# Probabilities times values in pairs of float16, in a two-layer attention and recurrence trunk on one Trainium2 core

## The chip, the cores and the metric

The kernel runs on one core of a Trainium2 chip. The metric is the device time of one execution in microseconds (us). Five engines work side by side, each with its own queue of instructions: TensorE (PE in the profile; its weight loads are PEld), VectorE (DVE), ScalarE (ACT), GpSimd (POOL) and SyncE (SP), which here only issues transfers.

## The reference

A sequence of 512 tokens with 16 meta tokens ahead of it (528 in all, width 2048) goes through an even layer (a convolution module and sparse attention side by side, then one output projection) and an odd layer (a gated linear recurrence). The change lies in the attention. For each of 8 heads, and for blocks of 128 queries:

```python
score = einsum('bqh,bqhs->bqs', wi_b, relu(dots))            # the indexer
_, idx = top_k(where(admissible, score, NEG_INF), topk)      # 128 keys for each query
logits = einsum('bqhc,bqkc->bhqk', q_b, c_sel) + bias
p = softmax(where(valid, logits, NEG_INF), axis=-1)
o = einsum('bhqk,bqkc->bhqc', p, c_sel)                      # probabilities times values
...
b_out = einsum('bthc,hcd->bthd', o_lat, w_uv) * silu(gate_b)
y = concatenate([a_out, b_out]) @ w_out
```

The kernel multiplies the latent keys by the up-projections first, so that each head has keys and values of width 128, and keeps the selection as a mask over all keys up to the block's chunk.

## The kernel before

A float32 operand is split into two float16 tiles, a high half (scaled, by ScalarE) and a low half (the rest, by VectorE, which therefore waits for the high half), and a main product is three float16 matmuls into the same PSUM tile: high by high, high by low, low by high. `products` (lines 214 to 216) does this for the projections; I call its three matmuls a main triple. Weights come in tiles of 2048 columns (`load_two`): SyncE loads `w`, ScalarE makes `wh` (L174), VectorE makes `wl` (L175), with three buffers each. Some weights are sums formed in DRAM by GpSimd's transfers (`ws`, L287 and L289), which are issued a few at a time behind steps of the attention.

The even layer runs through the table `EVEN`: `g` is a stripe of the convolution module, `s` a pair of indexer heads, `k` the selection of 128 keys for one block, `h` an attention head, `n` the layer norm. For head `h`, `head` computes gate and query, and every second head `keys_values` makes keys and values for two heads: five blocks of keys (the 16 meta keys, and four of 128), six float16 matmuls each, into one PSUM tile of 256 columns, 128 for each head, from which ScalarE evicts one head at a time (L555) into `Vt`.

`attend` then takes four blocks of queries, t = 0 to 3. For each, `softmax` makes the scores (L717), adds the bias and takes the extreme (L720, VectorE), takes the exponential (L724) and divides by the sum (L727, both ScalarE). The probabilities are transposed by TensorE in blocks of 128 keys into one PSUM tile for the t + 1 blocks (L736) and another for the meta keys (L740), evicted by ScalarE (L737, L741) into `pt` in float32, and multiplied by the values in float32 (L743), t + 2 products into `o`. After four blocks VectorE multiplies `o` by the gate (L754), and SyncE stores the result to `mbd` in DRAM (L755). `attend_meta` does the same for the meta queries of all heads at once (L679, L681).

Behind the eighth head come eight more gates (`GA`), and then the output projection, whose operands B21 and B22 are the heads' results read back from `mbd` (L852) and split (L234, L235; `fh`, `fl`).

Work is recorded in the order of the code, with priorities: `WGT` (weights) above `EVAC` (evictions of main products) above `SIDE` (attention) above `CONV` (the convolution's 31 steps on `z`, L632). A scheduler then sets each engine's order from its own estimates of times, so that a change in one part moves others. Each engine works strictly in its order.

Of the kernel before, what the change touches and what calls it, by code (L numbers as in the profile page):

```python
# [19 lines left out]
NM = 16  # L20
# [15 lines left out]
LEVELS = (1, 2, 4, 8, 16, 32, 64)  # L36

KS, QS = 2.0 ** 14, 1.0
WS = 2.0 ** 10
IW = 1.0 / WS  # L40

EROLE = {"gt": "em", "gb": "em", "qh": "em", "rstd": "em", "u": "em",
         "z": "ec", "acc": "ec", "sq": "ec",
         "Kh": "ek", "Vt": "ek",
         "wiT": "ei", "ki": "ei", "rt": "ei", "m8": "ei",
         "mask0": "ei", "mask1": "ei", "mask2": "ei", "mask3": "ei"}

# [27 lines left out]
def trunk_kernel(ctx: ExitStack, tc: tile.TileContext, x: bass.AP, w: bass.AP, wukv: bass.AP,  # L75
# [308 lines left out]
    def split_weights(s, half, part=None):  # L384

        m = KWM if s == S_KW else 128
        if s not in raw:
            raw[s] = raw_tile()
            if s == S_KW:
                first[s] = [[et([128, 5, 128], F32, *at).rearrange("p a b -> p (a b)").bitcast(F16)[:, :640]  # L390
                             for _ in range(2)] for at in (("Vt", 3), ("pt", 2))]
            else:
                first[s] = both_halves(*weight_tiles())
        hi, lo = first[s][half]
        w32 = raw[s][:, half * 1024:(half + 1) * 1024]
        cs = slice(0, 8 * m) if part is None else slice(4 * m * part, 4 * m * (part + 1))
        Q.dma_start(w32[:, cs], w[s, half, :, cs])
        in_turn("a", lambda: S.activation(hi[:, cs], w32[:, cs], AF.Copy, scale=WS))
        in_turn("v", lambda: V.scalar_tensor_tensor(lo[:, cs], w32[:, cs], WS, hi[:, cs],
                                                    op0=OP.mult, op1=OP.subtract))  # L400
# [124 lines left out]
    def keys_values(pr):  # L525
        with band(WGT):
            hi, lo = [E.tile([128, 2 * T], F16, name=n, bufs=1)[:, :1024] for n in ("uh", "ul")]
            split2(hi, lo, kvw.pop(), WS)
        Ks = []
        for hh in range(2):  # L530
            Kh = et([128, T], F32, "Kh", 3)
            for half in range(2):
                sl = slice(half * HT, half * HT + HT)
                p = ps1()
                n = 0
                for k in range(2):
                    ws = slice((2 * hh + k) * 128, (2 * hh + k + 1) * 128)
                    for a, b in ((hi, 0), (hi, 1), (lo, 0)):
                        P.matmul(p[:, :HT], a[:, ws], CX[k][b][:, sl], start=n == 0, stop=n == 5)
                        n += 1  # L540
                S.activation(Kh[:, sl], p[:, :HT], AF.Copy, scale=128.0 ** -0.5 * IW)
            Ks.append(Kh)
        Vs = [et([128, 5, 128], F32, "Vt", 3) for _ in range(2)]
        for Vh in Vs:
            G.memset(Vh[:, 0, :], 0.0)
        for i, (s0, ns) in enumerate(blocks):
            p = ps1()
            n = 0
            for k in range(2):
                ws = slice(512 + k * 256, 512 + (k + 1) * 256)  # L550
                for a, b in ((hi, 0), (hi, 1), (lo, 0)):
                    P.matmul(p[:ns, :256], CX[k][b][:, s0:s0 + ns], a[:, ws], start=n == 0, stop=n == 5)
                    n += 1
            for hh in range(2):
                S.activation(Vs[hh][:ns, i, :], p[:ns, hh * 128:(hh + 1) * 128], AF.Copy, scale=IW)  # L555
        if pr < HB // 2 - 1:
            load_keys_values(pr + 1)
        return Ks, Vs


    M = []
# [90 lines left out]
    def meta_tiles():  # L652

        t = epools["ei"].tile([128, 4, 128], F32, name="ql", bufs=1)
        for i, name in enumerate("qkvg"):
            meta[name] = t[:, i, :]
        meta["b"] = epools["ei"].tile([128, 128], F32, name="wiT", bufs=1)
        with band(SIDE):
            G.memset(meta["b"], NEG)
            for h in range(HB):  # L660
                G.dma_start(meta["b"][h * NM:(h + 1) * NM, h * NM:(h + 1) * NM], bias_rows(h, 0, NM, 0, NM))

    def attend_meta():

        e = et([128, T], F32, "sq", 3)
        L = e[:, :128]
        st = et([128, 4], F32, "st", 3)
        p = ps1()
        P.matmul(p[:, :128], meta["q"], meta["k"], start=True, stop=True)
        V.tensor_tensor_reduce(L, p[:, :128], meta["b"], -1.0, BIG, OP.add, OP.min, st[:, 0:1])  # L670
        S.activation(L, L, AF.Exp, bias=st[:, 0:1], scale=-1.0, accum_out=st[:, 2:3])
        V.reciprocal(st[:, 3:4], st[:, 2:3])
        S.activation(L, L, AF.Identity, scale=st[:, 3:4])
        p = ps1()
        P.transpose(p[:, :128], L, ident)
        pt = et([128, 5, 128], F32, "pt", 2)
        S.activation(pt[:, 0, :], p[:, :128], AF.Copy)
        p = ps1()
        P.matmul(p[:, :128], meta["v"], pt[:, 0, :], start=True, stop=True)  # L679
        mb = spare()  # L680
        V.tensor_tensor(mb[:, :128], p[:, :128], meta["g"], op=OP.mult)  # L681
        Q.dma_start(mbd[:, :, :NM].rearrange("h p t -> p h t"), mb[:, :128].rearrange("p (h t) -> p h t", h=HB))

    biased = {}
# [12 lines left out]
    def attend(h, qh, gb, Kh, Vt):  # L697
        o = pso()
        both = E.tile([128, 2 * T], F16, name=("uh", "ul")[h % 2], bufs=1)
        kr = both[:, :T], both[:, T:]  # L700
        both = (et([128, CW - 1 + T], F32, "u", 2) if h >= HB - 2 else et([128, T], F32, "acc", 2)).bitcast(F16)
        qr = both[:, :SEQ], both[:, SEQ:2 * SEQ]
        split2(*kr, Kh)
        split2(*qr, qh[:, NM:])

        def softmax(t, nq, q0, W):
            if h == 0:
                bias_ahead(h, t)
                some_steps(gsteps, 6, mask_ahead(h, t))
            e = biased.pop((h, t))  # L710
            L = e
            st = et([128, 4], F32, "st", 3)
            parts = ((0, W),) if W <= 512 else ((0, HT), (HT, W))
            for i, (s0, s1) in enumerate(parts):
                p = ps1()
                for a, b in ((0, 0), (0, 1), (1, 0)):
                    P.matmul(p[:nq, :s1 - s0], qr[a][:, q0 - NM:q0 - NM + nq], kr[b][:, s0:s1],  # L717
                             start=a + b == 0, stop=a == 1)

                V.tensor_tensor_reduce(L[:nq, s0:s1], p[:nq, :s1 - s0], e[:nq, s0:s1], -1.0,  # L720
                                       st[:nq, i - 1:i] if i else BIG, OP.add, OP.min,
                                       st[:nq, i:i + 1])
            i = len(parts) - 1
            S.activation(L[:nq, :W], L[:nq, :W], AF.Exp, bias=st[:nq, i:i + 1], scale=-1.0,  # L724
                         accum_out=st[:nq, 2:3])
            V.reciprocal(st[:nq, 3:4], st[:nq, 2:3])
            S.activation(L[:nq, :W], L[:nq, :W], AF.Identity, scale=st[:nq, 3:4])  # L727
            return L

        for t in range(NB):  # L730
            q0, W = NM + 128 * t, wk(t)
            L = softmax(t, 128, q0, W)
            pt = et([128, 5, 128], F32, "pt", 2)
            p = ps1()
            for j in range(t + 1):
                P.transpose(p[:, j * 128:(j + 1) * 128], L[:, NM + 128 * j:NM + 128 * (j + 1)], ident)  # L736
            S.activation(pt[:, 1:t + 2, :], p[:, :128 * (t + 1)], AF.Copy)  # L737

            p = ps1()
            P.transpose(p[:, :128], L[:, :128], ident)  # L740
            S.activation(pt[:, 0, :], p[:, :128], AF.Copy)  # L741
            for j in range(t + 2):
                P.matmul(o[:, 128 * t:128 * (t + 1)], Vt[:, j, :], pt[:, j, :],  # L743
                         start=j == 0, stop=j == t + 1)
            if h < HB - 1:
                behind = bias_ahead(h + 1, t)
                if t:
                    mask = mask_ahead(h + 1, t - 1)
                    behind = behind if h else mask
                some_steps(steps, (2, 2, 2, 3)[t] if h == 0 else (2, 2, 1, 2)[t] if h < 6 else 1, behind)  # L750
                if t == NB - 1:
                    mask_ahead(h + 1, t)
        mb = spare()
        V.tensor_tensor(mb[:, NM:], o, gb[:, NM:], op=OP.mult)  # L754
        Q.dma_start(mbd[h, :, NM:], mb[:, NM:])  # L755

    def head(h):
# [14 lines left out]
        with band(SIDE):  # L772
            for name, src in (("q", qh), ("k", Kh), ("g", gb)):
                S.activation(meta_of(name, h), src[:, :NM], AF.Copy)
            moved = G.dma_start(meta["v"][h * NM:(h + 1) * NM, :], Vt[:NM, 0, :])
            if h == HB - 1:
                some_steps(gsteps, 7, moved)
            if h == HB - 1:
# [896 lines left out]
```

## Time and profile before

| | us |
|---|---|
| median of 3 runs | 1742.28 |
| lowest, highest | 1742.22, 1743.06 |
| the profiled execution | 1739.7 |
| its span in the trace | 1737.9 |
| busy in the span: PE, PEld, DVE, ACT, POOL | 1720.5, 1457.2, 1401.3, 949.5, 271.3 |

The granted TensorE clock is 0.998 over the span. Lines of the page and of the trace name an instruction by its source line, its engine and its tiles, written as out<-in; buffer numbers are left out. Idle time of an engine that nobody waits for costs nothing.

### The profile page before, as it was taken

What the parts mean: (1) busy time and instruction counts of PE and PEld (TensorE: products, weight loads), DVE (VectorE), ACT (ScalarE), POOL (GpSimd) and SP (SyncE); (2) the same over time, 40 slices, a digit from 0 to 9 for tenths busy, and PEclk for the clock granted to TensorE, in tenths of its full rate; (3) what the DMA queues carried; (4) which work ended last, traced back from release to release, by engine and by line L of the source; (5) the groups of instructions that cost most, each with busy time, mean ns of one, the idle gap of its engine ahead of it and who ended that gap; (6) DMA issues with size and microseconds to landing.
All of it is one profiled execution on the core that took longest, in us unless ns stands there. A gap on an engine that the chain in (4) does not pass through costs nothing.

```text
span 1737.9 us, 38189 instructions
## 1 busy us (share of the span) xinstructions
PE 1720.5 (99%) x15784; PEld 1457.2 (84%) x15784; DVE 1401.3 (81%) x2362; ACT 949.5 (55%) x1745; POOL 271.3 (16%) x485
## 2 busy tenths in 40 slices
PE   9999999999999999999999999999999999999997
PEld 8775588888888888888888888899989989857886
DVE  7699899999569569689876667888878787759876
ACT  7333542224544555466644355778767777646553
POOL 1021233113343212010200111111111010000000
PEclk9999999999999999999999999999999999999999
DMA  9579677979999957887789987665555554424764
GB/s 368 150 253 262 193 236 186 263 206 243 246 245 303 219 192 251 252 285 260 228 287 309 297 269 242 190 181 172 141 176 157 153 165 134 123 85 170 255 223 141
DMA packets 103870, 378.53 MB, mean 218 GB/s; under 512 B 14096, under 2 KB 21944, under 8 KB 101840
## 3 DMA queue, kind: packets, MB, share of 16 engines
q1 hardware_dynamic: 70496, 232.68, 38.0%
q0 software_dynamic: 32912, 143.23, 33.9%
q8 instruction: 123, 2.02, 0.5%
q14 instruction: 51, 0.42, 0.1%
q10 hardware_dynamic: 288, 0.19, 0.0%
HBM read 354.26 MB, written 136.53 MB: 282 GB/s over the span
## 4 chain that ended last, share of the span: by engine, by line
PE 83%; DVE 10%; issue 3%; DMA 3%; ACT 1%; POOL 0%; SPq 0%; DVEq 0%; POOLq 0%; ACTq 0%
PE mps L216 18%; PE mps L214 18%; PE mps L215 18%; PE s L216 2%; PE s L215 2%; PE s L214 2%; DVE wl L175 2%; DVE z L632 2%; DVE mask L606 1%; PE sv L216 1%; PE sv L215 1%; PE sv L214 1%; PE po L743 1%; DVE m L605 1%; PE st L216 1%
## 5 line engine op out<-in xcount | busy, mean ns | idle before, releaser
L215 PE MATMUL mps<-xl,wh 128*128 128x264 f16 (+2 forms) x2840 | 806.0, 284 | 0.1
L216 PE MATMUL mps<-xh,wl 128*128 128x264 f16 (+2 forms) x2840 | 805.9, 284 | 0.1
L214 PE MATMUL mps<-xh,wh 128*128 128x264 f16 (+2 forms) x2840 | 805.8, 284 | 0.0
L175 DVE SCALAR_TENSOR_TENSOR wl<-w,wh 128x2048 f16<-128x2048 f32 (+1 forms) x188 | 429.1, 2282 | 136.6 <-ACT wh L174 136.1
L174 ACT ACTIVATE wh<-w 128x2048 f16<-128x2048 f32 (+1 forms) x188 | 357.6, 1902 | 304.1 <-PE mps L215 197.7
L216 PEld LDWEIGHTS <-wl 128*128 128x128 f16 x4184 | 409.4, 98 | 81.0 <-DVE wl L175 2.3
L215 PEld LDWEIGHTS <-wh 128*128 128x128 f16 x4184 | 409.4, 98 | 77.8 <-issue 0.6
L214 PEld LDWEIGHTS <-wh 128*128 128x128 f16 x4184 | 409.3, 98 | 77.6 <-issue 0.4
L632 DVE SCALAR_TENSOR_TENSOR z<-u,vec,z 128x528 f32<-128x528 f32 x240 | 179.5, 760 | 2.1
L289 POOL DMA_DIRECT2D ws<-in_w_dram x116 | 105.1, 1110 | 113.8 <-DMA ws<-ws 64.7
L216 PE MATMUL s<-xh,wl 128*128 128x256 f16 (+1 forms) x288 | 78.8, 274 | 0.0
L214 PE MATMUL s<-xh,wh 128*128 128x256 f16 (+1 forms) x288 | 78.8, 274 | 0.0
L215 PE MATMUL s<-xl,wh 128*128 128x256 f16 (+1 forms) x288 | 78.8, 274 | 0.0
L1242 ACT ACTIVATE kt1h<-k 128x512 f16<-128x512 f32 x64 | 41.2, 644 | 31.3 <-DVE k L1309 22.8
L1309 DVE TENSOR_TENSOR k<-k,e 128x512 f32<-128x512 f32 (+1 forms) x80 | 55.7, 696 | 1.4
L695 POOL DMA_DIRECT2D L<-mask x32 | 30.0, 939 | 160.0 <-DMA L<-bdram 89.5
L1243 DVE TENSOR_TENSOR kt1l<-k,kt1h 128x512 f16<-128x512 f32 x64 | 44.0, 687 | 12.1 <-ACT kt1h L1242 11.9
L222 DVE SCALAR_TENSOR_TENSOR gt<-mps,rstd 128x264 f32<-128x264 f32 (+1 forms) x70 | 31.3, 447 | 25.5 <-PE mps L216 24.5
L1243 DVE TENSOR_TENSOR kt0l<-k,kt0h 128x512 f16<-128x512 f32 x48 | 33.9, 707 | 17.7 <-ACT kt0h L1242 17.6
L724 ACT ACTIVATE L<-L,st 128x144 f32<-128x144 f32 (+3 forms) x32 | 18.4, 574 | 50.5 <-DVE st L720 50.2
L287 POOL DMA_DIRECT2D ws<-ws x58 | 36.5, 649 | 60.6 <-DMA ws<-in_w_dram 55.1
L1242 ACT ACTIVATE kt0h<-k 128x512 f16<-128x512 f32 x48 | 32.8, 683 | 17.7 <-DVE k L1309 17.2
(637 smaller groups left out, 3208.3 us busy)
## 6 DMA issues: line engine op xcount, KB each, us to landing
w<-in_w_dram SPq DMA_DIRECT2D x86, 1024.0 KB, 7.3
ws<-in_w_dram POOLq DMA_DIRECT2D x158, 512.0 KB, 7.9
w<-ws SPq DMA_DIRECT2D x116, 512.0 KB, 4.9
w<-in_w_dram SPq DMA_DIRECT2D x90, 512.0 KB, 4.8
ws<-ws POOLq DMA_DIRECT2D x58, 512.0 KB, 5.2
ws<-in_w_dram SPq DMA_DIRECT2D x16, 512.0 KB, 7.9
on<-h1d SPq DMA_DIRECT2D x30, 256.0 KB, 5.3
sq<-mbd POOLq DMA_DIRECT2D x16, 264.0 KB, 4.3
```

Of the source, the lines that this page charges most:

```text
L174: halved[:] = [S.activation(hi[:, :n], w32[:, :n], AF.Copy, scale=WS), V.scalar_tensor_tensor(lo[:, :n], w32[:, :n], WS, hi[:, :n], op0=OP ...
L175: V.scalar_tensor_tensor(lo[:, :n], w32[:, :n], WS, hi[:, :n], op0=OP.mult, op1=OP.subtract)]
L214: P.matmul(o, hi[:, ws], xh, start=start and k == 0, stop=False)
L215: P.matmul(o, hi[:, ws], xl, start=False, stop=False)
L216: issued.append(P.matmul(o, lo[:, ws], xh, start=False, stop=stop and k == len(X) - 1))
L222: V.scalar_tensor_tensor(dst[:, sl.start - o:sl.stop - o], p[:dst.shape[0]], IW, rstd[:dst.shape[0], sl], op0=OP.mult, op1=OP.mult)
L287: return (Q if m in (5, 7) and pair in EPAIRS else G).dma_start(dst, src)
L289: return G.dma_start(wsum[pair, m], src, accum_op=OP.add, max_dma_last_dim=4096)
L632: V.scalar_tensor_tensor(z, u[:, j:j + T], col(V_CW + i * CW + j), z, op0=OP.mult, op1=OP.add)
L1242: S.activation(hi, src, AF.Copy)
L1243: V.tensor_tensor(lo, src, hi, op=OP.subtract)
L1309: V.tensor_tensor(both, both, by, op=OP.mult)
```

## The change

Values are kept as two float16 tiles `Vh` and `Vl`, each of 256 columns for two heads, so one split evicts both heads at once. Probabilities are split at their eviction into `ph` and `pl`, scaled by 1024, which the outputs' eviction takes out again. Each float32 product becomes three float16 ones. For t = 0 to 2 the meta keys are transposed into the same PSUM tile as the others and share their eviction; for t = 3, which has 512 other columns, they keep their own. The meta queries' values are copied in two transfers for each head instead of one.

```diff
+PS = 2.0 ** 10
...
-        Vs = [et([128, 5, 128], F32, "Vt", 3) for _ in range(2)]
+        Vs = [et([128, 5, 256], F16, n, 2) for n in ("Vh", "Vl")]
...
-            for hh in range(2):
-                S.activation(Vs[hh][:ns, i, :], p[:ns, hh * 128:(hh + 1) * 128], AF.Copy, scale=IW)
+            split2(Vs[0][:ns, i, :], Vs[1][:ns, i, :], p[:ns, :256], IW)
...
-        return Ks, Vs
+        return Ks, [[t[:, :, hh * 128:(hh + 1) * 128] for t in Vs] for hh in range(2)]
...
-        pt = et([128, 5, 128], F32, "pt", 2)
-        S.activation(pt[:, 0, :], p[:, :128], AF.Copy)
+        ph, pl = [et([128, 5, 128], F16, n, 2)[:, 0, :] for n in ("ph", "pl")]
+        split2(ph, pl, p[:, :128], PS)
         p = ps1()
-        P.matmul(p[:, :128], meta["v"], pt[:, 0, :], start=True, stop=True)
+        vh, vl = meta["v"]
+        P.matmul(p[:, :128], vh, ph, start=True, stop=False)
+        P.matmul(p[:, :128], vh, pl, start=False, stop=False)
+        P.matmul(p[:, :128], vl, ph, start=False, stop=True)
         mb = spare()
-        V.tensor_tensor(mb[:, :128], p[:, :128], meta["g"], op=OP.mult)
+        V.scalar_tensor_tensor(mb[:, :128], p[:, :128], 1.0 / PS, meta["g"], op0=OP.mult, op1=OP.mult)
...
-            pt = et([128, 5, 128], F32, "pt", 2)
-            p = ps1()
-            for j in range(t + 1):
-                P.transpose(p[:, j * 128:(j + 1) * 128], L[:, NM + 128 * j:NM + 128 * (j + 1)], ident)
-            S.activation(pt[:, 1:t + 2, :], p[:, :128 * (t + 1)], AF.Copy)
-
-            p = ps1()
-            P.transpose(p[:, :128], L[:, :128], ident)
-            S.activation(pt[:, 0, :], p[:, :128], AF.Copy)
+            ph, pl = [et([128, 5, 128], F16, n, 2) for n in ("ph", "pl")]
+            lasts = [NM + 128 * j for j in range(t + 1)]
+            for j0, blks in ((0, [0] + lasts),) if t < NB - 1 else ((1, lasts), (0, [0])):
+                p = ps1()
+                n = len(blks)
+                for j, k0 in enumerate(blks):
+                    P.transpose(p[:, j * 128:(j + 1) * 128], L[:, k0:k0 + 128], ident)
+                split2(ph[:, j0:j0 + n, :], pl[:, j0:j0 + n, :], p[:, :128 * n].rearrange("p (n t) -> p n t", n=n), PS)
+            ot = o[:, 128 * t:128 * (t + 1)]
+            vh, vl = Vt
             for j in range(t + 2):
-                P.matmul(o[:, 128 * t:128 * (t + 1)], Vt[:, j, :], pt[:, j, :],
-                         start=j == 0, stop=j == t + 1)
+                P.matmul(ot, vh[:, j, :], ph[:, j, :], start=j == 0, stop=False)
+                P.matmul(ot, vh[:, j, :], pl[:, j, :], start=False, stop=False)
+                P.matmul(ot, vl[:, j, :], ph[:, j, :], start=False, stop=j == t + 1)
...
-        V.tensor_tensor(mb[:, NM:], o, gb[:, NM:], op=OP.mult)
+        V.scalar_tensor_tensor(mb[:, NM:], o, 1.0 / PS, gb[:, NM:], op0=OP.mult, op1=OP.mult)
...
-            moved = G.dma_start(meta["v"][h * NM:(h + 1) * NM, :], Vt[:NM, 0, :])
+            for part, Vp in zip(meta["v"], Vt):
+                moved = G.dma_start(part[h * NM:(h + 1) * NM, :], Vp[:NM, 0, :])
```

The orders of all engines differ from the first head up to the beginning of the output projection, and are the same from there on. Two places show how. The first is TensorE's order at the last block of the last head (t = 3): transposes out of `L`, main triples of a gate, and the products into `po`. Before:

```order
L216 MATMUL mps<-xh,wl 128x264
L736 MATMUL sv<-ident,L 128x128 x4
L740 MATMUL s_7191<-ident,L 128x128
...
L215 MATMUL mps<-xl,wh 128x264
L743 MATMUL po<-pt,Vt 128x128 x5
L216 LDWEIGHTS wl
```

And now (lines are numbered anew; L744 is the transpose, L749 to L751 are the products):

```order
L744 MATMUL sv<-ident,L 128x128 x4
L744 MATMUL s_7440<-ident,L 128x128
...
L749 LDWEIGHTS Vh
L749 MATMUL po<-ph,Vh 128x128
...
L750 LDWEIGHTS Vh
L750 MATMUL po<-pl,Vh 128x128
L751 LDWEIGHTS Vl
L751 MATMUL po<-ph,Vl 128x128
```

The products stood in one piece, 9 main triples behind the transposes; now the first stands 11.5 triples behind them and the other fourteen 7.5 further on. Counted from the start, 1345 main triples stood ahead of the last head's last product, and now 1365; the projection's first product follows 1440 triples in both.

The second place is VectorE's order from there to the projection's first weight tile. `kil` is the last head's output, `fl` the low halves of the projection's operands, `wl` those of weight tiles, of which the last in each list is the projection's first. Before:

```order
L754 TENSOR_TENSOR kil<-po,gb 128x512
L175 SCALAR_TENSOR_TENSOR wl<-w_8027,wh 128x2048
L644 SCALAR_TENSOR_TENSOR gb<-gb,gt 128x528
L235 SCALAR_TENSOR_TENSOR fl<-sq,fh 128x264 x6
L829 TENSOR_TENSOR z<-z,gb 128x528
L222 SCALAR_TENSOR_TENSOR gt<-mps,rstd 128x264
L828 SCALAR_TENSOR_TENSOR z<-gt,z 128x528
L235 SCALAR_TENSOR_TENSOR fl<-sq,fh 128x264 x6
L222 SCALAR_TENSOR_TENSOR gt<-mps,rstd 128x264
L175 SCALAR_TENSOR_TENSOR wl<-w_8443,wh 128x2048
```

And now (L176 is the weights' low half, L236 the split's, L761 the head's output):

```order
L176 SCALAR_TENSOR_TENSOR wl<-w_8287,wh 128x2048
L644 SCALAR_TENSOR_TENSOR gb<-gb,gt 128x528
L236 SCALAR_TENSOR_TENSOR pl<-sv,ph 128x512
L236 SCALAR_TENSOR_TENSOR pl<-s_7440,ph 128x128
L837 TENSOR_TENSOR z<-z,gb 128x528
L761 SCALAR_TENSOR_TENSOR kil<-po,gb 128x512
L236 SCALAR_TENSOR_TENSOR fl<-sq,fh 128x264 x2
L223 SCALAR_TENSOR_TENSOR gt<-mps,rstd 128x264
L236 SCALAR_TENSOR_TENSOR fl<-sq,fh 128x264 x4
L836 SCALAR_TENSOR_TENSOR z<-gt,z 128x528
L223 SCALAR_TENSOR_TENSOR gt<-mps,rstd 128x264
L176 SCALAR_TENSOR_TENSOR wl<-w_8703,wh 128x2048
```

The last head's output moved behind the previous weight tile, and of the sixteen `fl` out of heads' results six now stand ahead of the projection's first weight tile, where twelve did; the other ten follow it. On SyncE's queue, each head's store to `mbd` has one more weight tile's load ahead of it than before, two of them two more.

More of the change, by code (lines that the diff above doesn't have):

```diff
@@ L43 @@
          "z": "ec", "acc": "ec", "sq": "ec",
-         "Kh": "ek", "Vt": "ek",
+         "Kh": "ek", "Vh": "ek", "Vl": "ek",
          "wiT": "ei", "ki": "ei", "rt": "ei", "m8": "ei",
@@ L389, in split_weights @@
             if s == S_KW:
-                first[s] = [[et([128, 5, 128], F32, *at).rearrange("p a b -> p (a b)").bitcast(F16)[:, :640]
-                             for _ in range(2)] for at in (("Vt", 3), ("pt", 2))]
+                first[s] = [[et([128, 5, c], F16, n, 2).rearrange("p a b -> p (a b)")[:, :640] for n in names]
+                            for names, c in ((("Vh", "Vl"), 256), (("ph", "pl"), 128))]
             else:
@@ L656, in meta_tiles @@
             meta[name] = t[:, i, :]
+        both = meta["v"].bitcast(F16)
+        meta["v"] = both[:, :128], both[:, 128:]
         meta["b"] = epools["ei"].tile([128, 128], F32, name="wiT", bufs=1)
```

## The prediction

> **What bounds the kernel now.** I read the head of the page first, for the busy shares. Its times are in us.
>
> ```profile
> span 1737.9 us, 38189 instructions
> PE 1720.5 (99%) x15784; PEld 1457.2 (84%) x15784; DVE 1401.3 (81%) x2362; ACT 949.5 (55%) x1745; POOL 271.3 (16%) x485
> ```
>
> TensorE (PE) is idle for 17.4 us of 1737.9, so the time falls by what TensorE need no longer do and rises by each new wait of TensorE. Busy there means that some matmul is in flight, so the price of a matmul has to be read from starts. Next the busy times by stretch: attention runs from 230 to 632 us, and the last stretch holds the start of the even output projection.
>
> ```profile
> core 0: us, PE busy (x) PEld busy (x) DVE busy (x) ACT busy (x) POOL busy (x), PEclk, DMA share, GB/s
> 230.00:450.00 220.00, 218.25 (x1934) 189.66 (x1933) 215.13 (x435) 74.61 (x142) 60.87 (x90) 1.00 0.85 228
> 450.00:520.00 70.00, 70.00 (x624) 61.78 (x623) 39.79 (x78) 34.32 (x79) 26.92 (x41) 1.00 0.99 252
> 520.00:585.00 65.00, 65.00 (x573) 56.59 (x572) 51.73 (x77) 37.02 (x76) 19.03 (x33) 1.00 0.96 280
> 585.00:645.00 60.00, 60.00 (x535) 53.10 (x535) 32.37 (x67) 30.41 (x64) 14.48 (x24) 1.00 0.72 193
> 645.00:705.00 60.00, 60.00 (x536) 52.19 (x534) 59.41 (x112) 34.88 (x59) 10.74 (x20) 1.00 0.72 249
> ```
>
> TensorE is full in all five and its granted clock is 1.00. VectorE (DVE) is full in the first (215 of 220 us) and in the last (59.4 of 60), and has room between them. Then the waits of TensorE from 200 to 720 us: in all, times, longest.
>
> ```profile
> PE st L717 <- DVE st L720: 0.9, 1, 0.9
> PE s L736 <- ACT L L727: 0.5, 1, 0.5
> PE sv L736 <- ACT L L727: 0.3, 1, 0.3
> ```
>
> Only 1.7 us of waits lie here, so there is little to win beyond the matmuls themselves, and something to lose.
>
> **The products.** These rows of the timeline give start, duration, and how many instructions follow each other; between two starts lies the real price.
>
> ```profile
> L743 PE MATMUL po<-pt,Vt 128*128 128x128 f32 x224 | 30.2, 275 | 0.0
> 629.56 1.28 PE L743 MATMUL po<-pt,Vt 128*128 128x128 f32 x10
> 630.67 0.28 PE L216 MATMUL mps<-xh,wl 128*128 128x264 f16 x1
> 378.80 0.35 PE L717 MATMUL s<-ul,acc 128*128 128x144 f16 x3
> 378.99 0.28 PE L214 MATMUL mps<-xh,wh 128*128 128x264 f16 x1
> 1098.77 0.19 PE L1185 MATMUL s<-kt0l,kt0h 128*128 128x64 f16 x1
> 1098.80 0.19 PE L1186 MATMUL s<-kt0h 128*128 128x64 f16 x1
> 1098.77 0.10 PEld L1186 LDWEIGHTS <-kt0h 128*128 128x128 f16 x1
> ```
>
> A float32 product shows as two records: 224 records are the 112 products of the eight heads, (2+3+4+5) x 8, and the meta queries add one. Five of them take 630.67 - 629.56 = 1.11 us, or 0.222 us each, so 113 x 0.222 = 25.1 us go. In their place stand 339 float16 products of 128 columns, a form that the trace lacks. Nearest is the scores' group of three with 144 columns, in the same pattern (one stationary operand twice, another once): 378.99 - 378.80 = 0.19 us. Scaled to 128 columns that is 0.167 us for three. The other neighbour is 0.03 us for 64 columns; twice that, with two fixed costs, is 0.06, or 0.18 for three. I take 0.167, as 144 is far closer: 113 x 0.167 = 18.9 us come, and 25.1 - 18.9 = 6.2 us are saved; with 0.18 it would be 4.7 us. All of it counts, because TensorE is full where these products stand. The transposes stay float32 and as many.
>
> A weight load takes 0.10 us in the last row, as long as two such products. If loads set the pace, three would cost 0.30 us and the change would lose 339 x 0.10 - 25.1 = 8.8 us. That end I keep only as a rival: the rows of 64 columns start 0.03 us apart, each with its own load of 128 columns. The Trainium skill, TensorE: Matmul & The Clock Gate, Back-to-back issue gap, speaks against the change: it gives about 81 ns for each matmul of 128 columns in a stream of weight loads and matmuls. By that the new products would take 339 x 0.081 = 27.5 us, and the change would lose 2.4 us. The trace disagrees: 144 columns in such a stream take 63 ns here.
>
> **What VectorE gets.** Each group of probabilities, and each eviction of values, is now split by ScalarE (ACT) into the high half and by VectorE into the low half.
>
> ```profile
> 634.30 2.14 DVE L235 SCALAR_TENSOR_TENSOR fl<-sq,fh 128x264 f16<-128x264 f32 x6
> 119.39 0.67 DVE L580 SCALAR_TENSOR_TENSOR ql<-mps,ul 64x512 f16<-64x512 f32 x1
> 119.99 0.75 DVE L632 SCALAR_TENSOR_TENSOR z<-u,vec,z 128x528 f32<-128x528 f32 x1
> L775 POOL DMA_DIRECT2D ql<-Vt x8: 492/523/842, 243.5 to 554.7; - x8
> ```
>
> Such a low half costs 2.14 / 6, some 0.35 us, for 264 columns from SBUF, and 119.99 - 119.39 = 0.60 us for 512 from PSUM. On that line a head's groups of 256, 384, 512, 512 and 128 columns cost about 0.34 + 0.47 + 0.60 + 0.60 + 0.21 = 2.2 us, eight heads 17.8 us; 20 low halves of values cost 20 x 0.34 = 6.8 us. VectorE gets about 25 us. Its idle time by the table is 4.9 us before 450, then 30.2, 13.3 and 27.6 up to 645: 76 us. The convolution (L632), which has the lowest priority, moves out of the full first stretch into the free ones. So I cost these 25 us at nothing as throughput; if the cover were gone, what came late would be the low halves of weights (L175) and the evictions of main products (L222), for which TensorE waits.
>
> ScalarE loses: 64 evictions of probabilities become 40, 40 of values become 20 of twice the width. It is 34% to 57% busy in these stretches and nothing waits on it long, so this is worth nothing. GpSimd (POOL) issues eight more copies of meta values at 0.52 us: 4.2 us beside 60.87 of 220 busy, in front of mask additions (L695). TensorE's waits above name no DMA, so nothing again. The two evictions of outputs (L754, L681) become another operation over the same columns, at the same price.
>
> **The new wait, and the new order.** A product now waits for the low half on VectorE as well as for the high half on ScalarE. The scheduler answers by putting the products later behind their transposes: at the last group of head 7 the first stood nine main triples behind them, and now 11.5, with the rest seven or eight behind that. Main products fill the room. What this delays is the last head's result, which goes through VectorE, a store, a load and a split into the projection's operands:
>
> ```profile
> 630.87 0.69 DVE L754 TENSOR_TENSOR kil<-po,gb 128x512 f32<-128x512 f32 x1 [1.24 <-PE po L743]
> 631.48 2.28 DVE L175 SCALAR_TENSOR_TENSOR wl<-w,wh 128x2048 f16<-128x2048 f32 x1
> 631.59 0.33 SPq L755 DMA_DIRECT2D mbd<-kil  x1
> 639.59 0.73 ACT L234 ACTIVATE fh<-sq 128x264 f16<-128x264 f32 x2 [5.66 <-DMA sq<-mbd]
> 647.89 1.45 DVE L235 SCALAR_TENSOR_TENSOR fl<-sq,fh 128x264 f16<-128x264 f32 x4
> 662.51 0.28 PE L214 MATMUL mps<-fh,wh 128*128 128x264 f16 x1
> 674.78 2.28 DVE L175 SCALAR_TENSOR_TENSOR wl<-w,wh 128x2048 f16<-128x2048 f32 x1
> 678.71 0.28 PE L214 MATMUL s<-fh,wh 128*128 128x264 f16 x1
> ```
>
> The last four operands are done at 649.3, 13 us before the projection's first product at 662.51. In TensorE's order head 7 now ends 20 main triples later (1365 stand before it, where 1345 did); a triple is three matmuls of 0.112 us, so that is 6.7 us. The operands keep 6 us of lead and do not stop TensorE themselves. But VectorE has no idle time from 645 to 705, and the low halves of the projection's weights stand in its queue: the one that ends at 674.78 + 2.28 = 677.06 belongs (counting tiles of 16 triples) to the product that starts at 678.71, 1.65 us later, the thinnest lead that I found. Ahead of the projection's first weight tile stood 12 low halves of attention output, and now 6; six more go behind it (2.1 us), and the loads before them may come up to 3 us late, an estimate: half of the 5.66 us for which ScalarE waited for such a load. So VectorE may be 2 to 5 us late against a lead of 1.65 us, while later work of the same stretch can slip. TensorE may lose 0 to 3.5 us; I take 1.0. The sum is -6.2 + 1.0 = -5.2 us. The profiled execution took 1739.7 us, which becomes 1734.5. The median of the runs shown, 1742.28, stands 2.6 us above it; I carry the change over: 1737.1.
>
> On SP's queue one more weight tile is loaded ahead of each head's store. The loads there wait for a tile buffer, and for the last head's the buffer is free when the weights' low half ends at 631.48 + 2.28 = 633.8. The head's output comes 6.7 us later than 630.87, so this costs nothing.
>
> **The rivals.** 0.2% is 3.5 us, about what a measurement of this kernel can tell from no change: faster lies below 1738.8, slower above 1745.8.
>
> 1. The products' gain stays, less 0 to 2.6 us, or with up to 2 us of old waits gone: 1734 to 1738.8.
> 2. The handover to the projection takes more. For it speaks VectorE at 99% there; against it, that the operands still lead by 6 us. If VectorE's whole 6.7 us of delay showed beyond the 1.65 us of lead, 5.1 us would go: 1741.2. With a second such place it is 1743.
> 3. VectorE is late in the first stretch, where it is 98% busy: a low half stuck behind one of weights (2.28 us) holds up the products, with all main products queued behind them. Against it, the order leaves a product's low half some 6 us. If 12 groups of the first three heads waited 0.5 us each, the gain would be gone: 1742. If all 40 groups waited 0.25 us on average, 10 us, it would be slower: 1746.
> 4. The other side: weight loads set the products' pace. The place is each of the 339 products and the price the 0.10 us of the load's row, which gives the 8.8 us above: 1751. The gain is gone from 25.1 / 339 = 0.074 us per product, and from (25.1 + 3.5) / 339 = 0.084 us it is slower by over 0.2%. The starts 0.03 us apart speak against it. The Trainium skill's 81 ns, cited above, would give 1744.7.
>
> **How the numbers follow.** Case 1 gets 0.63, case 2 0.20, case 3 0.12, case 4 0.05. Faster is case 1: 0.63. The same: nearly all of case 2 (0.18), two thirds of case 3 (0.08), a little of case 4, where the price is between (0.02): 0.28. Slower is the rest: 0.09. The range takes all of case 1 and case 2 up to 1743, and with that the 4.7 us end of the product's price: 1734 to 1743 leaves out some 2 in 10.
>
> **What the profile of the changed kernel would show.** The rows po<-ph,Vh of 128x128 float16 start 0.056 us apart if the price is right; at 0.08 or more, case 4. Attention's float32 products are gone and VectorE has about 25 us more, with the stretch from 450 to 645 fuller. If TensorE waits for weights' low halves between 660 and 710 us, it is case 2; if for pl between 230 and 450, case 3. Wrong would be a TensorE idle time that rises by over 3 us elsewhere: later stages keep their order, but the transfers that prepare their weights are paced from here.

## The result, and the profile after

The changed kernel takes 1754.6 us (median of 5 runs, 1750.23 to 1755.16) against 1742.28 before: the ratio is 1.0069 (95% interval 1.0055 to 1.0082), so the change costs 12 us where I forecast a gain of 5.2. Its profiled execution took 1754.55 us with a span of 1752.8, 14.9 us above the span before.

From the head of the page of the kernel after:

```profile
span 1752.8 us, 38437 instructions
PE 1720.6 (98%) x15897; PEld 1453.4 (83%) x15897; DVE 1422.5 (81%) x2423; ACT 945.3 (54%) x1701; POOL 275.2 (16%) x493
```

TensorE's idle time rose from 17.4 to 32.2 us. The stretches of before again, now in the kernel after (the columns are those shown in the prediction):

```profile
230.00:450.00 220.00, 215.77 (x1939) 186.35 (x1937) 212.20 (x437) 67.28 (x108) 53.77 (x81) 0.99 0.80 213
450.00:520.00 70.00, 64.52 (x612) 55.82 (x609) 46.50 (x91) 31.70 (x65) 27.64 (x42) 0.98 0.94 233
520.00:585.00 65.00, 60.10 (x544) 51.32 (x542) 54.23 (x91) 27.58 (x52) 25.07 (x42) 0.97 1.01 291
585.00:645.00 60.00, 59.92 (x566) 52.55 (x564) 38.87 (x81) 40.41 (x78) 15.08 (x23) 1.00 0.86 220
645.00:705.00 60.00, 60.00 (x544) 52.29 (x542) 53.73 (x105) 34.35 (x64) 11.73 (x22) 1.00 0.65 224
```

The time is lost between 230 and 585 us, inside attention; from 585 to 705 us TensorE is full, and the handover to the projection that I watched is clean. The longest of TensorE's waits from 200 to 720 us (in all, times, longest):

```profile
PE sv L744 <- ACT L L732: 5.5, 1, 5.5
PE st L722 <- DVE st L725: 3.9, 2, 2.6
PE po L750 <- DVE pl L236: 3.0, 2, 2.7
PE sv L722 <- DVE st L725: 2.0, 1, 2.0
```

Before, 1.7 us of waits stood here. The names are ScalarE's and VectorE's, but they only hand on a wait. VectorE's own waits from 390 to 645 us begin, in the kernel after, with

```profile
DVE L L725 <- DMA L<-mask: 18.5, 5, 7.1
```

and in the kernel before no such group is in that list. The longest wait of TensorE, followed back through the chain of waits (start, duration, engine, tile, line):

```profile
464.22 6.24 DMA L<-bdram
470.51 0.49 issue
471.01 8.51 DMA L<-mask
479.68 0.43 DVE L L725
480.12 0.63 DVE gb L644
480.78 0.22 ACT ql L781
480.99 0.53 ACT L L732
481.56 0.48 PE sv L744
```

This is the last block of head 3. Its bias is loaded from DRAM into a buffer `L` (L696), the mask is added there by a second transfer (L700), and only then may VectorE take up the scores (L725). GpSimd issues both, the second when the first has landed. All three buffers `L` are in use, so the load of head h+1's block begins when head h's block has been transposed out of its buffer. It began at 464.2 us and was ready at 479.5; VectorE had waited 7.07 us, and everything behind it in its queue waited too:

```profile
479.68 0.43 DVE L725 CUSTOM_DVE_ANT_0 L<-s,L 128x264 f32<-128x264 f32 x1 [7.07 <-DMA L<-mask]
```

For the ledgers below I call **stall** what lies between the starts of two neighbouring matmuls beyond their usual distance (0.112 us for 264 columns, others in proportion), counted where it is over 0.04 us. It contains the waits and the half-speed matmuls behind them. Stalls were 17.6 us before and are 38.55 after. Span less stalls is 1720.3 before and 1714.25 after. So TensorE's own work fell by 6.05 us, as forecast (6.2), and 20.95 us of stalls came, of which 19.4 lie between 200 and 700 us.

### The profile page after: what moved, and what is told of

Same layout as the page of the kernel before. It is cut to its first block, busy times and chain, and to the rows that moved or that the text cites. A ratio compares the mean times of both kernels' runs of the same rounds, so it can differ in the third digit from the quotient of the medians.

```text
span 1752.8 us, 38437 instructions
## 1 busy us (share of the span) xinstructions
PE 1720.6 (98%) x15897; PEld 1453.4 (83%) x15897; DVE 1422.5 (81%) x2423; ACT 945.3 (54%) x1701; POOL 275.2 (16%) x493
## 4 chain that ended last, share of the span: by engine, by line
PE 78%; DVE 11%; DMA 5%; issue 5%; ACT 1%; POOL 1%; SPq 0%; DVEq 0%; POOLq 0%; ACTq 0%
PE mps L217 17%; PE mps L216 17%; PE mps L215 17%; PE s L217 2%; PE s L215 2%; PE s L216 2%; DMA L<-mask 2%; DVE wl L176 2%; DVE z L632 2%; DVE mask L606 2%; DMA L<-bdram 1%; PE sv L217 1%; PE sv L215 1%; PE sv L216 1%; DVE m L605 1%
## 5 line engine op out<-in xcount | busy, mean ns | idle before, releaser
L176 DVE SCALAR_TENSOR_TENSOR wl<-w,wh 128x2048 f16<-128x2048 f32 (+1 forms) x188 | 429.1, 2283 | 134.5 <-ACT wh L175 134.1
L700 POOL DMA_DIRECT2D L<-mask x32 | 32.4, 1022 | 155.2 <-DMA L<-bdram 81.6
L1251 DVE TENSOR_TENSOR kt0l<-k,kt0h 128x512 f16<-128x512 f32 x48 | 34.0, 708 | 17.7 <-ACT kt0h L1250 17.6
```

What stands on the lines that cost most here:

```text
L176: V.scalar_tensor_tensor(lo[:, :n], w32[:, :n], WS, hi[:, :n], op0=OP.mult, op1=OP.subtract)]
L1251: V.tensor_tensor(lo, src, hi, op=OP.subtract)
```

## The experiments

Sixteen runs of fifteen kernels, in four groups. Theory A is the one above: bias and mask of a block land too late behind three buffers. Theory B is that VectorE, full up to 450 us, is late with the low halves. Theory C is that the scheduler made another order and any order costs something at random. A block's **lead** is the time from the landing of its mask to its use. Every ratio is to the kernel before, run beside it.

### More buffers, no low halves, the evictions alone

`more_L` is the changed kernel with more buffers:

```diff
...
-        e = et([128, W], F32, "L0", 1) if t == 0 else et([128, T], F32, "L", 3)
+        e = et([128, W], F32, "L0", 2) if t == 0 else et([128, T], F32, "L", 6)
```

> The changed kernel with six buffers L instead of three and two L0 instead of one, so that the bias and mask of the next head's blocks can be fetched before the present head has given its buffers back. Theory A (TensorE waits because bias and mask land just in time behind late buffers): the waits of 5.5, 2.0 and 2.7 us around 480 to 552 us and two of the three stretches at half clock go; 1754.6 falls to 1740 to 1745, with the wait at 385 us (last block of the selection) left. Theory B (VectorE's low halves overload the stretch 230 to 450 us): at most 2 us are won, 1752 to 1755. Theory C (every other order by the scheduler costs something, at random): any time from 1742 to 1760, and new waits at other places.

1745.61 us, 1.0026 (1.0016 to 1.0035): by the two ratios, 7.5 us of the 12 came back. VectorE's waits for a mask from 390 us on shrank from 18.5 to 1.2 us. The wait at 385 us that I expected to stay is gone too, and a new one stands in head 0. TensorE's waits from 200 to 720 us begin with

```profile
PE s L744 <- ACT L L732: 8.5, 1, 8.5
```

It belongs to head 0's third block. In the chain of waits its mask (start, duration) is

```profile
327.45 9.43 DMA L<-mask
```

With three buffers this mask landed 3.1 us after its issue at 326.0 us, and nobody waited. With six, another block's mask is issued just ahead of it, and a weight load of SyncE is in flight beside it (327.5 to 336.5 us).

`before_more_L` makes the same edit in the kernel before.

> The kernel before, with the same six L and two L0. Theory A: it waited 1.7 us in all in the attention, so it stays at 1740 to 1743. Theory C: another order, so 1745 or more.

1743.85 us, 1.0012 (1.0003 to 1.0021), 0.85 us above theory A's range. The buffers alone are no gain: the kernel before had no such waits to lose, and its head 0 got a 2.6 us wait.

`no_low_halves` is the changed kernel with VectorE's halves left out: values and probabilities keep only high halves, and all three products take these, so its output is another.

```diff
...
-            split2(Vs[0][:ns, i, :], Vs[1][:ns, i, :], p[:ns, :256], IW)
+            S.activation(Vs[0][:ns, i, :], p[:ns, :256], AF.Copy, scale=IW)
...
-                split2(ph[:, j0:j0 + n, :], pl[:, j0:j0 + n, :], p[:, :128 * n].rearrange("p (n t) -> p n t", n=n), PS)
+                S.activation(ph[:, j0:j0 + n, :], p[:, :128 * n].rearrange("p (n t) -> p n t", n=n), AF.Copy, scale=PS)
```

> The changed kernel without the low halves of probabilities and values: the same three float16 products, all of the high halves, so TensorE's work is the same and VectorE's some 25 us less (the output loses precision). Theory B: the added time goes, 1735 to 1739. Theory A: bias and mask still come late, but the wait at 385 us goes: 1746 to 1752. Theory C: anything up to 1760.

1758.18 us, 1.0093 (1.0077 to 1.011). Theory B falls as the main cause: VectorE lost all 21.4 us of its new work and the loss stayed, 6 us above the range that I gave for theory A. VectorE waited 22.3 us for masks from 390 to 645 us.

`merged_only` is the kernel before with nothing but the shared evictions, in float32 and with float32 products.

```diff
-        Vs = [et([128, 5, 128], F32, "Vt", 3) for _ in range(2)]
+        Vs = et([128, 5, 256], F32, "Vt", 2)
...
+            lasts = [NM + 128 * j for j in range(t + 1)]
+            for j0, blks in ((0, [0] + lasts),) if t < NB - 1 else ((1, lasts), (0, [0])):
```

> The kernel before with the shared evictions alone: meta keys in the same PSUM tile for three of four blocks, values of two heads evicted together, all in float32 and with float32 products. Theories A and B: no low halves, so no more VectorE work and no later products: 1740 to 1744. Theory C, or if the shared evictions are what delays the buffers: 1746 or more.

1756.34 us, 1.0088 (1.0073 to 1.0103). The loss comes with the part of the change that I had costed at nothing, without any float16.

### Which eviction, and what the triples do alone

`meta_keys_only` has the second hunk of that diff alone, `value_pairs_only` the first.

> The kernel before with one thing of the change: for the first three blocks of a head the meta keys' transpose stands in the same PSUM tile as the other keys' and leaves with them in one eviction; values and products stay as before. Theory A1 (the shared eviction of the meta keys is what draws a head's blocks together, so that the bias and mask transfers behind the three L buffers land too late): 1752 to 1757 us, as with both shared evictions (1756.3). Theory A2 (it is the values' pairing that moves the work): 1740 to 1744 us here. Theory C (any new order falls at random between 1740 and 1757): no forecast.

> The kernel before with the other half of the shared evictions: values of two heads leave PSUM in one float32 eviction of 256 columns into a buffer of [128,5,256], two of them; meta keys' evictions and products stay as before. Theory A1: 1740 to 1744 us, since the blocks of a head are not drawn together. Theory A2: 1752 to 1757 us. If neither this nor the meta keys' eviction alone costs over 5 us, it takes both, or the order falls at random (C).

1757.84 us, 1.009 (1.0075 to 1.0105), and 1742.19 us, 1.0002 (0.9992 to 1.0011). So it is the meta keys' place in the shared PSUM tile. VectorE's waits for masks from 390 us on, first with the meta keys shared, then with the values paired:

```profile
DVE L L720 <- DMA L<-mask: 20.2, 10, 5.6
```

```profile
DVE L L718 <- DMA L<-mask: 2.0, 1, 2.0
```

Why an eviction does this shows in where the blocks stand. I counted the main triples that start before each block's scores are taken up:

| block | before | values paired | meta keys shared | after | triples alone |
|---|---|---|---|---|---|
| head 2, t = 0 | 889 | 889 | 880 | 936 | 949 |
| head 2, t = 3 | 918 | 919 | 890 | 948 | 987 |
| head 3, t = 0 | 925 | 925 | 919 | 988 | 994 |
| head 3, t = 3 | 970 | 970 | 950 | 1011 | 1049 |
| head 5, t = 3 | 1093 | 1093 | 1070 | 1135 | 1204 |
| head 7, t = 3 | 1316 | 1314 | 1292 | 1323 | 1345 |

The side work takes its PSUM tiles from a ring of four (`ps1`). A head took 13 of them (3, 3, 3 and 4 for its blocks) and takes 10 when blocks 0 to 2 share. The scheduler then draws the blocks together (that the ring is the reason is read from the code; no run changes its size): the four of head 2 stand within 10 triples (3.4 us at 0.336 us each) where they stood within 29 (9.7 us). But the loads behind them do not get shorter. In the kernel before, GpSimd issued the bias loads of head 3 like this:

```profile
427.76 0.57 POOL L691 DMA_DIRECT2D L<-bdram  x1 [9.10 <-issue]
...
431.41 0.56 POOL L691 DMA_DIRECT2D L<-bdram  x1
...
438.32 0.56 POOL L691 DMA_DIRECT2D L<-bdram  x1 [2.12 <-PE sv L717]
...
444.56 0.91 POOL L691 DMA_DIRECT2D L<-bdram  x1
```

and with the meta keys shared like this (the last load stands behind a mask's issue that waited in the same queue):

```profile
434.68 0.56 POOL L691 DMA_DIRECT2D L<-bdram  x1 [11.33 <-ACT L L724]
436.20 0.57 POOL L691 DMA_DIRECT2D L<-bdram  x1
...
439.34 0.56 POOL L691 DMA_DIRECT2D L<-bdram  x1 [0.69 <-issue]
...
447.52 0.85 POOL L695 DMA_DIRECT2D L<-mask  x1 [4.39 <-PE s L717]
448.31 0.63 POOL L691 DMA_DIRECT2D L<-bdram  x1
```

The first three start within 4.7 us instead of 10.6, and from a load's issue to its mask's landing it takes 10.9, 17.0 and 14.6 us instead of 6.5, 11.7 and 8.9. The leads of head 3 were 6.4, 7.5, 5.0 and 1.9 us before; here they are 2.0, 0.1, 0.1 and 0.1.

`triples_only` is the changed kernel with neither shared eviction: the meta keys have a tile of their own, and values are split one head at a time.

```diff
...
-            for j0, blks in ((0, [0] + lasts),) if t < NB - 1 else ((1, lasts), (0, [0])):
+            for j0, blks in ((1, lasts), (0, [0])):
```

> The changed kernel with its three float16 products but without the shared evictions: meta keys in a PSUM tile of their own for every block, values split one head at a time. Theory A (the shared evictions cost the 12 us): the products' gain of 6.2 us shows and the time is 1735 to 1741 us. Rival B2 (the products' shorter heads alone also make the L buffers' transfers late): 1744 to 1752 us. Rival of the selection (VectorE's extra low halves put the selection and with it head 0's last mask late): 1740 to 1744 us, with a stall of 2 to 8 us at 330 to 390 us into the span alone.

1751.25 us (1746.04 to 1753.11), 1.0049 (1.0031 to 1.0067): my theory missed. The gain of the products is there (span less stalls is 1714.1), and no wait for a mask is left from 390 us on, but 8.6 us of stalls stand between 600 and 650 us, and 2.9 between 550 and 600. By the table its blocks lie 255 triples apart from head 2 to head 5 (before 204): attention runs late, and the last head's last block comes 29 triples later. The stalls stand in head 7, whose first two blocks are taken up at 1328 triples (before at 1281 and 1294): from 618 to 628 us TensorE has no main triple between the attention's steps and waits at one after the other. 112 triples still follow before the projection; why none of them stands there was not followed.

`no_low_more_L` has the edits of `no_low_halves` and `more_L` together (output as in the former).

> The changed kernel with six L buffers and two L0 buffers, and without the low halves of probabilities and values (the three products are all of the high halves, so the output differs). If the 8.5 us stall at 340 us that stayed with more buffers alone (1745.6 us) comes from VectorE's extra work ahead of the selection, it is gone here: 1735 to 1739 us. If it comes from the order alone: 1743 to 1748 us.

1740.13 us, 0.999 (0.998 to 0.9999), 1.1 us above the range of the first reading; the wait in head 0 is halved:

```profile
PE s L745 <- ACT L L733: 4.3, 1, 4.3
```

So once the buffers are there, VectorE's low halves cost 1745.6 - 1740.1 = 5.5 us, and 8.5 - 4.3 = 4.2 us of that are this wait. The mask goes out 3.2 us earlier (324.3 us) and lands in 4.4 us instead of 9.4; no weight load of SyncE is in flight beside it here (none between 324.4 and 332.9 us). So it is less the low halves' amount than what they make meet; that the load slows the mask is argued from these times.

### The transfers themselves

`triples_more_L` is `triples_only` with the buffers of `more_L`; `meta_keys_more_L` is `meta_keys_only` with them.

> The changed kernel with its three float16 products, without the shared eviction of the meta keys and with the values split one head at a time, and with six L buffers and two L0 buffers. Theory A (what costs the time are bias and mask that land late behind three L buffers): the stalls behind landed masks past 390 us into the span are gone, and of the products' 6.2 us what the selection's late stall leaves: 1736 to 1742 us. Rival (the triples themselves cost time on TensorE in their order): 1746 to 1752 us, as without the buffers (1751.3).

> The kernel before with the meta keys' shared eviction and with six L buffers and two L0 buffers. Theory A: the 15.8 us that the shared eviction cost alone (1757.8) go, but for a stall in head 0, which the buffers cannot help: 1740 to 1746 us, and no lead of a block of heads 1 to 7 below 5 us. Rival (the shared eviction costs by its size or by its PSUM tile, with no transfer in it): 1752 to 1758 us.

1754.43 us, 1.007 (1.0056 to 1.0083), a miss: the triples alone have no late transfers from 390 us on, so buffers do not help there, and head 0 gets the new wait of the kernels with six buffers (7.0 us). From 585 to 645 us TensorE is busy for 52.5 of 60:

```profile
585.00:645.00 60.00, 52.50 (x465) 43.85 (x463) 39.04 (x89) 37.44 (x83) 9.21 (x18) 0.97 0.63 183
```

The other came out as expected: 1745.95 us, 1.002 (1.001 to 1.003), 12 us below the same kernel with three buffers, and every lead of heads 1 to 7 is 8 us or more.

`before_mask_twice` issues each mask transfer twice in the kernel before (a masked score stays masked, and no compute engine has more to do).

```diff
+        G.dma_start(biased[h, t][:, :wk(t)], M[t], accum_op=OP.add)
         return G.dma_start(biased[h, t][:, :wk(t)], M[t], accum_op=OP.add)
```

> The kernel before with each mask transfer issued twice, the second behind the first, so that each block's bias and mask take some 7 us longer to land; nothing is added on a compute engine. Theory A (the chain of bias and mask behind three L buffers is the scarce thing, and before had leads of 0 to 8 us in heads 3 and 5): stalls of 2 to 7 us in head 0, 1, 3 and 5, and 1752 to 1775 us. Rival (the transfers are not what sets the time): 1741 to 1745 us.

1796.36 us, 1.0306 (1.0288 to 1.0324), more than I expected. TensorE's stalls rise from 17.6 to 69.0 us, with span less stalls at 1720.4 as before; VectorE's waits from 390 us on:

```profile
DVE L L721 <- DMA L<-mask: 38.7, 9, 13.0
```

In heads 3 and 5 the chain had little slack before the change: leads of 0.1 to 7.5 us.

`four_L` is the changed kernel with four buffers `L` instead of three.

> The changed kernel with four L buffers instead of three and one L0 buffer. Theory A: one buffer more lets the transfers of a block begin one block sooner, some 3 to 6 us, about as much as the leads lack: 1742 to 1750 us, with fewer stalls behind landed masks than the changed kernel's. Rival (any order by the scheduler falls at random): anything from 1740 to 1757 us with leads that do not tell the time.

1737.66 us, 0.998 (0.9971 to 0.9989): below my expectation and below both kernels.

### What was still open

`after_mask_head_0` is the changed kernel with three buffers, but without the mask transfers of heads 1 to 7 (whose scores so stay unmasked).

```diff
     def mask_ahead(h, t):
...
+        if h:
+            return None
         return G.dma_start(biased[h, t][:, :wk(t)], M[t], accum_op=OP.add)
...
```

> The changed kernel with three L buffers as it has them, but with the mask transfer left out for heads 1 to 7 (their scores are not masked, so the output differs); only head 0's blocks are masked. Theory A: without the second transfer a block's bias has landed 6 to 9 us earlier, the stalls behind it in heads 3 and 5 are gone, and what is left is the selection's stall in head 0: 1736 to 1743 us. Rival C (the order, not the transfers, costs the time): no reason to come below 1748 us.

1734.52 us, 0.9957 (0.9942 to 0.9972), 1.5 us below theory A's range. The order is nearly that of the kernel after (head 2's blocks at 933 to 945 triples, head 3's last at 1002, against 936 to 948 and 1011), and the stalls of 200 to 700 us fall from 23.1 to 6.7 us. TensorE's waits there:

```profile
PE st L723 <- DVE st L726: 3.4, 1, 3.4
PE s L593 <- DMA ul<-ql: 0.2, 1, 0.2
```

That decides between A and C: the drawn-together order costs little when the second transfer is gone. It also moves fewer bytes, so its 0.4% is no version to use.

`triples_no_low` is `triples_more_L` without low halves (as in `no_low_halves`).

> The kernel with triples alone and six L buffers (1754.4 us, with 8.7 us of stalls from 590 to 630 us into the span), now without low halves of probabilities and values: the three products are all of the high halves, and the output differs. If the stalls ahead of the output projection come from VectorE's second half of each eviction, which keeps the PSUM tiles longer, they are gone: 1738 to 1744 us. If they come from the number of PSUM tiles alone (13 a head in a ring of four): they stay, 1746 to 1752 us.

1739.7 us, 0.9987 (0.9978 to 0.9996), and the stalls from 550 to 650 us are gone. So it is the low halves that made attention late there. I read it as the second half of each eviction: of a head's 13 PSUM tiles, the eight that take transposes wait for ScalarE and then for VectorE. That is not shown apart from the rest, for the same edit takes 24.5 us of work off VectorE and sends head 0's last mask out at 372.7 instead of 383.6 us. In the changed kernel the shared eviction seems to take this pressure away, and to put it on the transfers.

`four_L_again` and `five_L`:

> The changed kernel with four L buffers once more, in more rounds. 1737.7 us was measured, ratio 0.998 (0.9971 to 0.9989). Theory A: the products' gain less the stalls that are left, 1736 to 1740 us. If the first result was chance: 1741 to 1744 us.

> The changed kernel with five L buffers and one L0 buffer. Theory A: the leads of heads 3 and 5 grow further, and the head 0 stall behind the selection's mask is what decides: 1735 to 1745 us; as good as four buffers if loads that start earlier do not slow head 0's masks, and 3 to 8 us worse if they do, as with six (1745.6 us, whose head 0 mask took 9.4 us to land against 4.7 with four).

1738.63 us, 0.9978 (0.9968 to 0.9988), and 1740.91 us, 0.9998 (0.999 to 1.0007). Four buffers hold on a second chip. TensorE's waits from 200 to 720 us with four:

```profile
PE sv L722 <- DVE st L725: 1.1, 1, 1.1
PE st L722 <- DVE st L725: 0.5, 1, 0.5
PE s L593 <- DMA ul<-ql: 0.3, 1, 0.3
PE po L750 <- DVE pl L236: 0.3, 1, 0.3
```

With five, VectorE waits 6.7 us for masks, among them that of head 5's first block, whose buffer `L0` is still single here; with six, head 0's mask is late. Why five is no better than four was not followed further.

The ledger over the profiled executions, in us:

| kernel | span | stalls | span less stalls | VectorE's waits for masks, 390 to 645 |
|---|---|---|---|---|
| before | 1737.9 | 17.6 | 1720.3 | none |
| values paired | 1739.5 | 19.2 | 1720.3 | 2.0 |
| meta keys shared | 1756.5 | 36.2 | 1720.3 | 20.2 |
| after | 1752.8 | 38.55 | 1714.25 | 18.5 |
| after, six L | 1743.3 | 29.1 | 1714.2 | 1.2 |
| triples alone | 1750.8 | 36.7 | 1714.1 | none |
| after, four L (second run) | 1734.4 | 20.3 | 1714.1 | 3.0 |
| before, mask twice | 1789.4 | 69.0 | 1720.4 | 38.7 |

## Why the prediction was wrong

**The products' price: right.** The new products start 0.055 to 0.06 us apart, also behind a weight load each. This is the timeline of the kernel after:

```profile
456.35 0.22 PE L750 MATMUL po<-pl,Vh 128*128 128x128 f16 x1
456.40 0.22 PE L751 MATMUL po<-ph,Vl 128*128 128x128 f16 x1
456.46 0.22 PE L749 MATMUL po<-ph,Vh 128*128 128x128 f16 x1
456.52 0.22 PE L750 MATMUL po<-pl,Vh 128*128 128x128 f16 x1
```

Three take 0.17 us, as the term had it. The ledger gives 6.05 to 6.2 us less work in every kernel with triples. Rival 4 is out: a load of 0.10 us does not set the pace. Neither do the 81 ns of the Trainium skill (TensorE: Matmul & The Clock Gate, Back-to-back issue gap).

**The handover: not needed.** I charged 1.0 us there, and there is no wait between 660 and 710 us. Rival 2 did not show in any kernel with triples: none has a stall from 655 to 715 us. Where the triples stand without the shared eviction, attention itself is late and waits inside head 7, not at the handover.

**VectorE's 25 us: nearly right as throughput, wrong as time.** It got 21.2 us. What it delays is the selection: head 0's last mask went out at 378.1 us instead of 367.0, and TensorE waited 2.6 us for it. The waits for `pl` that rival 3 expected came to 3.0 us, two in number, not 40 small ones; the longer stood behind a late mask and a weight's low half in VectorE's queue.

**The step that failed** is the term of the shared eviction. I counted it for ScalarE alone, "nothing waits on it long, so this is worth nothing"; alone in the kernel before it costs 15.8 us. With it failed the sentence on GpSimd, "TensorE's waits above name no DMA, so nothing again", which left out the wait that came. In the sum I put new waits at 1.0 us; 20.95 us of stalls came. A list of TensorE's waits names only the last in the chain, and shows a wait only once it has come. The quantity to read was how long each block's mask had landed before its use: in head 5 of the kernel before, 4.2, 5.7, 1.4 and 0.1 us. That chain is a loop (use, transpose, load, mask, next use), so an order that draws four uses together uses up its slack even though nothing was added to it. The order of before and after showed that in heads 2 to 4 (head 3's four blocks lie within 23 triples, before within 45); I compared it at the last head only. My own condition, "TensorE idle time that rises by over 3 us elsewhere", is what happened. With a fourth buffer, which the forecast did not have, the sum nearly comes out: by the ratios the gain is 3.5 to 3.8 us, and 5.2 were forecast.

## What to carry to other kernels

Before trusting a saving on a full engine, list for each buffer that is refilled behind its use how long the refill has landed before it is needed, and cost every reordering against that lead, in transfers that run at once and not one by one. A cheaper step can lose time by letting its neighbours run closer together; if the saving is in the trace but not in the time (span less stalls fell by 6 us here), look for the loop that ran dry and give it one more buffer. More is not better: here four beat three, five, and six (these with a second `L0`).

## What was not expected of the hardware

A wait of TensorE can cost more than its own length. With the three longest waits of the kernel after (2.63, 5.48 and 2.67 us of idle time) its clock stood at half for a while; the columns are again those of the stretches:

```profile
385.30:388.71 3.41, 3.41 (x18) 2.39 (x18) 3.41 (x5) 0.83 (x2) 0.81 (x1) 0.50 1.06 205
388.71:390.00 1.29, 1.29 (x13) 1.13 (x12) 1.29 (x3) 0.00 (x0) 0.52 (x1) 1.00 1.05 206
```

3.41 us at half speed is, as an estimate, 1.7 us lost on top of the 2.63; after idle times of 1.3 to 2.0 us this kernel's clock stayed full. The length alone does not decide it. In `five_L` an idle time of 1.78 us (from 817.4 us) was followed by half clock, and in `before_mask_twice` one of 2.56 us (from 416.0 us) was not. In the eighteen traces each stretch of half clock between 200 and 900 us lasted 3.41, 6.83 or 10.24 us. If a trace is cut into steps of 3.41 us from its first change of clock on, every step at full clock with over 2.0 us of TensorE's idle time in it was followed by half clock, none with under 1.75 us was, and between these both occurred; the 2.56 us lay across two steps, 1.8 and 0.7. The Trainium skill (TensorE: Matmul & The Clock Gate, HAM oscillation — how this bites in real kernels) puts the limit of an idle gap at about 3.4 us; by these runs 1.78 us can be enough.
